# RWKV time mixing on one core: a second GpSimd product for each early unit, and the mix vectors transposed between two halves of unit 0

## The chip, the core and the metric

The kernel runs on one core of a Trainium2 chip. A core has five engines with a queue of instructions each: PE (TensorE, the matrix engine, with its weight loads shown as PEld), DVE (VectorE), ACT (ScalarE), POOL (GpSimd) and SP (SyncE, which only issues DMAs here). They run side by side and wait for one another through semaphores. The metric is the device time of one execution in microseconds (us); lower is better.

## What is computed

For x of shape 16 x 2048 x 256 and with x_prev the same rows shifted by one position in the sequence (zero in front), the reference is, cut to what reaches the output:

```python
xv = x * time_mix_v + x_prev * (1 - time_mix_v)
xr = x * time_mix_r + x_prev * (1 - time_mix_r)
v = xv.reshape(-1, d_model) @ value_weight
r = xr.reshape(-1, d_model) @ receptance_weight
out = ((1.0 / (1.0 + np.exp(-r))) * v) @ output_weight
```

The key path (time_mix_k, key_weight) is computed in the reference but its result isn't used, and the kernel leaves it out.

## The kernel before

The 16 x 2048 rows are cut into 64 units of 512 rows, four to a batch element ("batch" below). All work is on x transposed: the 256 features lie on the 128 partitions in two halves, called ko 0 and ko 1, and the 512 rows of a unit lie along the free dimension.

Mixing is rewritten so that it costs little: with c = 1/time_mix - 1, the mix is time_mix * (c * x_prev + x), and time_mix is multiplied into the weights once, at the start. For each unit and for each of R (m = 0) and V (m = 1) there remain two **products**, c * x_prev for ko 0 and for ko 1 (128x512 each; `scale` on DVE, line 258, `scale_pool` on POOL, line 268, `scale_act` on ACT, line 515), and one **sum** over both halves (`add`, 128x1024, DVE, line 280). The shifted x_prev is the transposed x one slot earlier; the first slot of a unit (or of a batch) has to be filled by a small copy, `wrap_slots` (lines 427 and 428).

The loop over g at line 523 does, for unit g, on PE: R's four matmuls (`project`, line 288, into psum_r), transposes of later units (line 209, 8 for each unit, into ps_t), V's four matmuls (line 288, into psum_v), and the eight output matmuls of the unit before (line 312, into psum_o). psum_v has one buffer. ACT takes the sigmoid of psum_r (line 536), copies transposed tiles from ps_t (line 225) and the output from psum_o (line 346). DVE multiplies the sigmoid with psum_v into z_sb (line 581). Beside this each engine prepares the mix of later units.

The order is written out by hand: the framework adds semaphores but moves nothing. Tables filled in lines 483 to 510 say in which iteration which piece is made:

- `sums[g]`: DVE's sums ahead of the z_sb product of iteration g. The last of these is `last`.
- `held[g]`: DVE's sums behind the z_sb product of iteration g.
- `products[g]`: DVE's products ahead of the sums.
- `pooled[g]`: pieces whose second product (ko 1) POOL does. They are issued after the z_sb product in program order, and made to wait for `last` (`scale_pool(p, last)`, line 589, with the reason "one at a time").

For units 3 to 7, R's sum is in `sums` of the iteration before the unit, and V's is in `held` there (unit 7: both in `sums`). Before the change, DVE makes three of the four products of each of units 3 to 8 in the iteration before (both of R, the first of V; for unit 8's R two iterations before), and POOL makes V's second product one iteration earlier still. Unit 2's V gets its second product from ACT (line 564). From unit 10 on (`PAIRS`), two units are mixed together, and POOL makes the second product of both R and V as 128x1024; this stays as it is.

In the steady order DVE runs, per iteration: products, R's sum of unit g + 1, z_sb of unit g, V's sum of unit g + 1. PE's V matmuls of unit g + 1 need that last sum. POOL runs, per iteration: the wrap copy of unit g + 2 (line 428), the second product (line 268), then the issue of a load of x (line 114) and a two-column copy (line 427).

At the start, PE runs 21 matmuls on zeros (line 153), a 4x128 transpose of the mix vectors (`coefficients`, line 171), the transposes of unit 0 in two halves (line 232; the half with the later rows first, into psum_r, the other into psum_v), 10 more matmuls on zeros, and then unit 0. DVE turns the transposed mix vectors into time_mix, 1 - time_mix and c (lines 175 to 184), copies unit 0's shifted slot (line 239), and scales the weights (lines 455, 462, 471).

Of the kernel before, what the change touches and what calls it, by code (L numbers as in the profile page):

```python
# [15 lines left out]
def kernel(  # L16
# [44 lines left out]
    START_T = [1, 3, 5, 6, 7, 9, 11, 12]  # L61
    AHEAD = 6
    PAIRS = 10
    WARM = 21
    WARM2 = 10

    consts = ctx.enter_context(tc.tile_pool(name="consts", bufs=1))
# [11 lines left out]
    SYNC = mybir.DependencyInfo(mybir.DependencyClass.Sync, mybir.DependencyReason.DATA)  # L79
# [70 lines left out]
    def warm_up(n):  # L150
        ps = ps_t_pool.tile([P, P], FP32, name="ps_t")
        for _ in range(n):
            nc.tensor.matmul(out=ps, lhsT=zeros, rhs=zeros, start=True, stop=True)  # L153

    warm_up(WARM)

# [12 lines left out]
    def coefficients():  # L169
        ps = ps_o_pool.tile([P, 2, KO], FP32, name="psum_o")  # L170
        nc.tensor.transpose(
            out=ps.rearrange("p m k -> p (m k)"), in_=tm_rows, identity=ident_f[: 2 * KO, : 2 * KO]
        )
        tm = consts.tile([P, 2, KO], FP32)
        nc.vector.tensor_copy(out=tm, in_=ps)
        nc.vector.tensor_scalar(
            out=tms, in0=tm, scalar1=0.0, scalar2=1e-30, op0=ALU.is_equal, op1=ALU.mult
        )
        nc.vector.tensor_tensor(out=tms, in0=tms, in1=tm, op=ALU.add)
        nc.vector.tensor_scalar(  # L180
            out=tm_prev, in0=tm, scalar1=-1.0, scalar2=1.0, op0=ALU.mult, op1=ALU.add
        )
        nc.vector.reciprocal(c_sb, tms)
        nc.vector.tensor_scalar(out=c_sb, in0=c_sb, scalar1=-1.0, scalar2=None, op0=ALU.add)

    coefficients()

    def by_dma(b, lo, hi, after=None):

        op = nc.sync.dma_start_transpose(  # L190
            out=xt[b][:, 1 + lo : 1 + hi].rearrange("p j k c -> p (j k) c"),
            in_=x_bf[b][:, lo:hi].rearrange("p j d -> p (j d)"),
        )
        if after is not None:
            tc.add_manual_dep(op.ins, after.ins.name, SYNC, reason="not beside a load")
# [31 lines left out]
    def first_transposes():  # L227
        def half(h, pool, name):
            ps = pool.tile([P, UJ, KO, P], FP32, name=name)
            for jj in range(H):  # L230
                for ko in range(KO):
                    nc.tensor.transpose(  # L232
                        out=ps[:, jj, ko],
                        in_=x_unit[:, 0, h * H + jj, ko * P : (ko + 1) * P],
                        identity=ident_f,
                    )
            nc.scalar.copy(out=xt[0][:, 1 + h * H : 1 + h * H + H], in_=ps[:, 0:H])
            if h == 1:
                nc.vector.tensor_copy(out=xt[0][:, 0, :, 1:P], in_=ps[:, H - 1, :, 0 : P - 1])

        half(1, ps_r_pool, "psum_r")
        half(0, ps_v_pool, "psum_v")

    def slots(piece, off=0):

        b, _, lo, hi = piece
        j = lo // P + (lo // TU if b < BYUNIT else 0) + off
        return slice(j, j + (hi - lo) // P)

    def mixed(piece):  # L250
        b, m, lo, hi = piece
        j = lo // P % (2 * UJ)
        return mix[(b * S + lo) // (2 * TU)][:, m, j : j + (hi - lo) // P]
# [9 lines left out]
                op0=ALU.mult,  # L263
            )

    def scale_pool(piece, after):
        b, m, _, _ = piece
        op = nc.gpsimd.tensor_scalar(  # L268
            out=mixed(piece)[:, :, 1],
            in0=xt[b][:, slots(piece), 1],  # L270
            scalar1=c_sb[:, m, 1:2],
            scalar2=1.0,
            op0=ALU.mult,
            op1=ALU.mult,
        )
        tc.add_manual_dep(op.ins, after.ins.name, SYNC, reason="one at a time")

    def add(piece):
        b = piece[0]
# [121 lines left out]
    def tile_for(b):  # L401

        if b not in mix:
            mix[b] = mixpool.tile([P, 2, 2 * UJ, KO, P], BF16, name="mix")

    def pieces(g):

        b, e = divmod(g, UB)
        tile_for(g // 2)
        return [(b, m, e * TU, (e + 1) * TU) for m in range(2)]  # L410
# [75 lines left out]
    pooled = {g: [] for g in range(-1, NU)}  # L486
# [12 lines left out]
    for u in range(2, NU):  # L499
        paired = u >= PAIRS  # L500
        if paired and u % 2:
            continue
        for m, (b, _, lo, hi) in enumerate(pieces(u)):
            w = first[u][m]
            group = (b, m, lo, hi + TU if paired else hi)
            if paired or m == 1 and w > 1 and u != PAIRS - 1:
                products[w].append((group, (0,)))
                pooled[w - 1].append(group)
            else:
                products[w].append((group, (0,) if u == 2 and m == 1 else (0, 1)))  # L510

    def scale_act(piece, kos):
        b, m, _, _ = piece
        for ko in kos:
            nc.scalar.activation(  # L515
                out=mixed(piece)[:, :, ko],
                in_=xt[b][:, slots(piece), ko],
                func=ACT.Copy,
                scale=c_sb[:, m, ko : ko + 1],
            )  # L520

    z_prev2 = z_prev = None
    for g in range(NU - 1):
        ps_r = ps_r_pool.tile([P, KO, TU], FP32, name="psum_r")
        if g == 0:
            project_unmixed(ps_r, 0)
            advance(1)
            project_unmixed(ps_r, 1)
            for ko in range(KO):
                wrap_slots(pieces(1)[0], ko)  # L530
                scale(pieces(1)[0], (ko,))
            last = add(pieces(1)[0])
        else:
            project(ps_r, g, 0)
        s_sb = zpool.tile([P, KO, TU], BF16, name="s_sb")
        nc.scalar.activation(out=s_sb, in_=ps_r, func=ACT.Sigmoid)  # L536
        advance(START_T[g] if g < len(START_T) else g + LOOK - (g == CROSS - 1))
        for b in range(B - 5, B):
            if g == max(UB * (b - 2) - 1, CROSS + (b > B - 5)):
                new_xt(b)  # L540
                if b == B - 5:
                    for pair in kept.pop(g):
                        store(nc.sync, *pair, after=half_load)
                    by_dma(b, J - UJ, J, last_load)
                    by_dma(b, 0, J - UJ, last_load)
                else:
                    by_dma(b, 0, J)
                for pair in kept.pop(g, []):
                    store(nc.sync, *pair)
            if g == UB * (b - 1) + 1:  # L550
                nc.scalar.copy(out=xt[b][:, 0, :, 1:P], in_=xt[b][:, J, :, 0 : P - 1])
        if LATE_O < g < NU - 2:
            output(g - 2, z_prev2)
        for p in products.get(g + 1, []):
            if g >= FREE and p[0][1] == 1:
                scale_act(p[0], (0,))
        for p in [q for q, _ in products[g]] + pooled[g]:
            last_unit_of = p[3] // TU - 1
            need = last_unit_of if p[0] < BYUNIT else min(last_unit_of + 1, UB - 1)
            assert UB * p[0] + need < tnext, (g, p, tnext)  # L560
            if g > AHEAD or p not in pooled[g]:
                wrap_slots(p)
        if g == 1:
            scale_act(pieces(2)[1], (1,))
        for p, kos in products[g]:
            if not (g - 1 >= FREE and p[1] == 1):
                scale(p, kos)
        for p in sums[g]:
            last = add(p)
        for p in pooled[g]:  # L570
            if p[0] >= BYUNIT:
                wrap_slots(p)
        ps_v = ps_v_pool.tile([P, KO, TU], FP32, name="psum_v")
        project(ps_v, g, 1)
        if g == 0:
            scale_act(pieces(1)[1], (0,))
            advance(2)
        z_sb = zpool.tile([P, KO, TU], BF16, name="z_sb")
        n = TU // 2 if g == NU - 2 else TU
        for c in range(0, TU, n):  # L580
            nc.vector.tensor_tensor(  # L581
                out=z_sb[:, :, c : c + n],
                in0=s_sb[:, :, c : c + n],
                in1=ps_v[:, :, c : c + n],
                op=ALU.mult,
            )
        for p in pooled[g]:
            wrap_slots(p, after=last)
            scale_pool(p, last)
        for p in held[g]:  # L590
            add(p)
        if z_prev is not None and not LATE_O <= g < NU - 3:
            output(g - 1, z_prev)
        if g == 1:
            advance(4)
        z_prev2, z_prev = z_prev, z_sb
# [31 lines left out]
```

## Time and profile before

| | |
|---|---|
| median of 4 runs | 203.15 us (202.12, 202.53, 203.76, 203.76) |
| the profiled execution's own time | 202.59 us |
| its span, first to last instruction | 200.5 us |
| granted TensorE clock over the span | 1.000 |
| DMA, mean | 286 GB/s |

The profile is of one execution. It has a page with the busy time of each engine, the chain of work that ended last and the costliest groups of instructions, and the trace behind it answers by view: the waits (who waited for whom), the timeline (instructions in order of time: start, duration, engine, line, operation, out<-in, shape, how many; in brackets the idle time in front and what ended it), the chain of waits in order of time, the DMA issues, and sums over windows. Times in the timeline count from the start of the span. Of a run of equal instructions the timeline gives one row, with the time from the first start to the last end. DVE starts an instruction some 0.08 us before the one in front is recorded as ended, so that spacing and duration differ.

### The profile page before, as it was taken

The numbers are of one execution on the slowest core, as the hardware profiler recorded it, in microseconds if no ns is written. First come the engines' busy times: TensorE is split into PE (matmuls) and PEld (weight loads), VectorE is DVE, ScalarE is ACT, GpSimd is POOL, SyncE is SP. The second block draws the span as 40 slices with busy tenths as digits, with TensorE's granted clock in tenths as the row PEclk, the third lists the DMA queues.
The fourth block names the chain that finished last, engine by engine and source line by source line (L and its number), as shares of the span: only waits on it lengthen the run. The fifth ranks groups of instructions, "written<-read, shape, count | busy, mean of one in ns | idle before, by whom it ended". The sixth has DMA issues, their size and how long they took to land.

```text
span 200.5 us, 3886 instructions
## 1 busy us (share of the span) xinstructions
PE 195.6 (98%) x1420; PEld 125.9 (63%) x1420; DVE 186.2 (93%) x296; ACT 180.1 (90%) x202; POOL 83.7 (42%) x115
## 2 busy tenths in 40 slices
PE   7999999999999999999999999999999999999993
PEld 6666675666666666666666666655666565555671
DVE  2799999999999999999999999999999999999982
ACT  3599899999999999999999999899999999999982
POOL 1656572443533534425434354443344444444200
PEclk9999999999999999999999999999999999999999
DMA  5999999999999999999999999899999999999575
GB/s 163 295 162 215 232 281 274 278 280 273 293 312 294 289 273 289 289 280 286 286 280 317 301 406 295 288 187 207 298 269 415 332 218 267 418 418 413 226 310 213
DMA packets 32298, 57.26 MB, mean 286 GB/s; under 512 B 21780, under 2 KB 23064, under 8 KB 28312
## 3 DMA queue, kind: packets, MB, share of 16 engines
q1 hardware_dynamic: 28208, 40.77, 59.1%
q0 software_dynamic: 3920, 16.12, 40.1%
q8 instruction: 11, 0.18, 0.3%
q10 hardware_dynamic: 152, 0.13, 0.2%
q14 instruction: 7, 0.06, 0.1%
HBM read 34.34 MB, written 33.55 MB: 339 GB/s over the span
## 4 chain that ended last, share of the span: by engine, by line
PE 88%; DVE 5%; ACT 3%; issue 2%; POOL 0%; DVEq 0%
PE psum_v L288 25%; PE psum_o L312 25%; PE psum_r L288 24%; PE ps_t L209 8%; DVE z_sb L581 2%; PE ps_t L153 2%; DVE mix L280 2%; PE ps_t L312 1%; ACT s_sb L536 1%; DVE mix L258 1%; PE psum_r L302 1%; ACT mix L515 1%; PE psum_v L232 1%; PE psum_r L232 1%; ACT xt L225 1%
## 5 line engine op out<-in xcount | busy, mean ns | idle before, releaser
L268 POOL TENSOR_SCALAR mix<-xt,c_sb 128x1024 bf16<-128x1024 bf16 (+1 forms) x55 | 61.0, 1109 | 92.6 <-DVE mix L280 81.9
L581 DVE TENSOR_TENSOR z_sb<-s_sb,psum_v 128x1024 bf16<-128x1024 bf16 (+1 forms) x64 | 76.8, 1201 | 3.5 <-PE psum_v L288 1.5
L280 DVE TENSOR_TENSOR mix<-mix,xt 128x1024 bf16<-128x1024 bf16 x112 | 77.0, 697 | 1.6
L288 PEld LDWEIGHTS <-w_bf 128*128 128x128 bf16 x516 | 48.7, 98 | 38.4 <-issue 0.7
L536 ACT ACTIVATE s_sb<-psum_r 128x1024 bf16<-128x1024 f32 x63 | 65.0, 1031 | 3.5 <-PE psum_r L288 2.7
L346 ACT COPY o_sb<-psum_o 128x1024 f32<-128x1024 f32 x60 | 61.1, 1018 | 7.1 <-PE psum_o L312 7.1
L288 PE MATMUL psum_v<-mix,w_bf 128*128 128x512 bf16 (+1 forms) x256 | 65.3, 377 | 0.3 <-DVE z_sb L581 0.2
L288 PE MATMUL psum_r<-mix,w_bf 128*128 128x512 bf16 (+1 forms) x252 | 64.2, 377 | 0.1
L312 PE MATMUL psum_o<-wo_bf,z_sb 128*128 128x256 bf16 x486 | 63.2, 272 | 0.0
L312 PEld LDWEIGHTS <-z_sb 128*128 128x128 bf16 x512 | 49.8, 98 | 20.4 <-issue 1.4
L225 ACT COPY xt<-ps_t 128x1024 bf16<-128x1024 bf16 x36 | 36.6, 1030 | 0.0
L209 PEld LDWEIGHTS <-x_bf 128*128 128x128 bf16 x328 | 21.4, 98 | 9.1 <-POOL xt_first L427 0.5
L209 PE MATMUL ps_t<-ident,x_bf 128*128 128x128 bf16 x328 | 24.5, 219 | 0.1
L258 DVE TENSOR_SCALAR mix<-xt,c_sb 128x1024 bf16<-128x1024 bf16 (+1 forms) x49 | 22.1, 459 | 0.0
L515 ACT ACTIVATE mix<-xt,c_sb 128x1024 bf16<-128x1024 bf16 x12 | 13.9, 1157 | 0.0
L280 DVE TENSOR_TENSOR mix<-mix,xt_first 128x1024 bf16<-128x1024 bf16 x15 | 10.6, 709 | 0.1
L114 POOL DMA_DIRECT2D x_bf<-in_x_dram x13 | 8.5, 656 | 0.0
L258 DVE TENSOR_SCALAR mix<-xt_first,c_sb 128x512 bf16<-128x512 bf16 x22 | 6.6, 348 | 0.2
L225 ACT COPY xt_first<-ps_t 128x1024 bf16<-128x1024 bf16 x5 | 5.2, 1036 | 0.0
L153 PE MATMUL ps_t<-zeros 128*128 128x128 bf16 x31 | 3.7, 311 | 1.0 <-DVE zeros L90 1.0
L268 POOL TENSOR_SCALAR mix<-xt_first,c_sb 128x512 bf16<-128x512 bf16 x6 | 4.1, 686 | 0.6
L428 POOL COPY xt_first<-xt_first 128x254 bf16<-128x254 bf16 x5 | 2.0, 393 | 5.5 <-DVE mix L280 5.4
(66 smaller groups left out, 52.1 us busy)
## 6 DMA issues: line engine op xcount, KB each, us to landing
out_dram<-o_sb SPq DMA_DIRECT2D x28, 1024.0 KB, 14.4
x_bf<-in_x_dram POOLq DMA_DIRECT2D x13, 1024.0 KB, 24.6
out_dram<-o_sb SPq DMA_DIRECT2D x4, 512.0 KB, 2.8
out_dram<-o_sb SPq DMA_DIRECT2D x6, 256.0 KB, 2.5
x_bf<-in_x_dram POOLq DMA_DIRECT2D x5, 256.0 KB, 7.1
o_sb<-in_x_dram SPq DMA_DIRECT2D x2, 512.0 KB, 5.3
x_bf<-in_x_dram POOLq DMA_DIRECT2D x2, 512.0 KB, 11.1
o_sb<-in_x_dram SPq DMA_DIRECT2D x2, 256.0 KB, 3.1
```

The lines of the kernel that those rows point to most:

```text
L114: return nc.gpsimd.dma_start(out=x_bf[b], in_=rows(b), max_dma_last_dim=run)
L209: nc.tensor.transpose(out=ps[:, jj], in_=src[:, jj, ko * P : (ko + 1) * P], identity=idn)
L225: nc.scalar.copy(out=xt[b][:, j0 : j0 + UJ], in_=ps)
L258: nc.vector.tensor_scalar(out=mixed(piece)[:, :, ko], in0=xt[b][:, slots(piece), ko], scalar1=c_sb[:, m, ko : ko + 1], scalar2=None, op0=A ...
L268: op = nc.gpsimd.tensor_scalar(out=mixed(piece)[:, :, 1], in0=xt[b][:, slots(piece), 1], scalar1=c_sb[:, m, 1:2], scalar2=1.0, op0=ALU.mul ...
L280: return nc.vector.tensor_tensor(out=mixed(piece), in0=mixed(piece), in1=xt[b][:, slots(piece, 1)], op=ALU.add)
L288: nc.tensor.matmul(out=ps[:, mo, :], lhsT=w_bf[:, m, ko, mo * P : (mo + 1) * P], rhs=mixed((b, m, e * TU + lo, e * TU + hi))[:, :, ko], st ...
L312: nc.tensor.matmul(out=ps[:, slot, :], lhsT=z[:, ko, jj * P : (jj + 1) * P], rhs=wo_bf[:, ko, :], start=(ko == 0), stop=(ko == KO - 1),)
L346: nc.scalar.copy(out=o_sb[b][:, j0 : j0 + UJ, :], in_=ps)
L515: nc.scalar.activation(out=mixed(piece)[:, :, ko], in_=xt[b][:, slots(piece), ko], func=ACT.Copy, scale=c_sb[:, m, ko : ko + 1],)
L536: nc.scalar.activation(out=s_sb, in_=ps_r, func=ACT.Sigmoid)
L581: nc.vector.tensor_tensor(out=z_sb[:, :, c : c + n], in0=s_sb[:, :, c : c + n], in1=ps_v[:, :, c : c + n], op=ALU.mult,)
```

## The change

Four edits:

1. For units 3 to 8, R's second product goes from DVE to POOL, ahead of V's second product in the same iteration (for unit 8 as the code says: in iteration 6, where V's of unit 8 also is).
2. Unit 2's V gets its second product from POOL instead of ACT, with no added wait on `last`.
3. `coefficients()` is called between the two halves of unit 0's transposes, instead of ahead of both. On DVE its instructions stay in the same order, ahead of the copy into unit 0's first slot.
4. 23 matmuls on zeros at the start in place of 21.

POOL's queue is then, in the iterations of units 2 to 5: wrap copy, R's second product, V's second product, issue of the load, two-column copy. In DVE's queue one `scale` is gone in each, and R's sum waits for POOL's product.

```diff
-    WARM = 21
+    WARM = 23
...
-    coefficients()
-
...
             nc.scalar.copy(out=xt[0][:, 1 + h * H : 1 + h * H + H], in_=ps[:, 0:H])
             if h == 1:
+                coefficients()
                 nc.vector.tensor_copy(out=xt[0][:, 0, :, 1:P], in_=ps[:, H - 1, :, 0 : P - 1])
...
-    def scale_pool(piece, after):
+    def scale_pool(piece, after=None):
...
-        tc.add_manual_dep(op.ins, after.ins.name, SYNC, reason="one at a time")
+        if after is not None:
+            tc.add_manual_dep(op.ins, after.ins.name, SYNC, reason="one at a time")
...
-            if paired or m == 1 and w > 1 and u != PAIRS - 1:
+            if paired or w > 1 and u != PAIRS - 1:
                 products[w].append((group, (0,)))
-                pooled[w - 1].append(group)
+                at = w if m == 0 and u == AHEAD + 2 else w - 1
+                pooled[at].insert(0 if m == 0 else len(pooled[at]), group)
             else:
                 products[w].append((group, (0,) if u == 2 and m == 1 else (0, 1)))
...
-            if g > AHEAD or p not in pooled[g]:
+            if g > AHEAD or p not in pooled[g] or p == pieces(AHEAD + 2)[0]:
                 wrap_slots(p)
         if g == 1:
-            scale_act(pieces(2)[1], (1,))
+            scale_pool(pieces(2)[1])
```

## The prediction

> **What bounds the kernel now.** I read the busy times first, then who waited for whom, then the timeline from 0 to 37 us.
>
> ```profile
> PE 195.6 (98%) x1420; PEld 125.9 (63%) x1420; DVE 186.2 (93%) x296; ACT 180.1 (90%) x202; POOL 83.7 (42%) x115
> ```
>
> ```profile
> PEld L288 <- DVE mix L280: 0.4, 2, 0.2
> ...
> PE psum_v L288 <- DVE z_sb L581: 0.2, 1, 0.2
> ```
>
> PE has work for 98% of the span, and its waits are short: a gain can come only from the few places where it stands still. The chain of waits has PE alone from 33.40 us on, with a V projection every 3.05 us (40.10, 43.15, 46.20). Before that the spacing shows the losses. An iteration with 8 transposes should take 3.05 us: the ones from 16.41 and from 19.66 take 3.25 (0.20 lost each), the one from 29.91 takes 3.49 (0.44 lost). One with 16 transposes takes 3.50 (22.91 to 26.42), without a wait. So 0.84 us is all that the product edits can win. The timeline shows what ends these waits:
>
> ```profile
> 21.63 0.68 POOL L268 TENSOR_SCALAR mix<-xt_first,c_sb 128x512 bf16<-128x512 bf16 x1
> 22.06 0.80 DVE L280 TENSOR_TENSOR mix<-mix,xt_first 128x1024 bf16<-128x1024 bf16 x1
> ...
> 22.78 0.88 DVE L258 TENSOR_SCALAR mix<-xt_first,c_sb 128x512 bf16<-128x512 bf16 x3
> 22.91 0.55 PEld L288 LDWEIGHTS <-w_bf 128*128 128x128 bf16 x4 [0.20 <-DVE mix L280]
> ...
> 23.04 0.20 POOL L427 COPY xt_first<-xt_first 128x2 bf16<-128x2 bf16 x1
> ...
> 25.61 0.69 DVE L280 TENSOR_TENSOR mix<-mix,xt_first 128x1024 bf16<-128x1024 bf16 x1
> ...
> 27.03 0.73 POOL L427 COPY xt_first<-xt_first 128x2 bf16<-128x2 bf16 x1
> 27.04 0.67 DVE L280 TENSOR_TENSOR mix<-mix,xt_first 128x1024 bf16<-128x1024 bf16 x1
> ...
> 33.40 1.02 PE L288 MATMUL psum_v<-mix,w_bf 128*128 128x512 bf16 x4 [0.25 <-DVE z_sb L581]
> ```
>
> DVE has no gap here; V's sum ends at 22.86 and PE goes on at 22.91. So DVE is the bound of these iterations. The second thing to see is that a DVE sum and a POOL operation take turns. The sum at 22.06 begins 0.25 us before POOL's product ends (22.31) and takes 0.80, not the 0.69 of 25.61, which meets no product: it ends 0.55 after the product. The sums at 15.52 and 28.76 end 0.54 after theirs. The other way round, POOL's two-column copy takes 0.20 at 23.04, but 0.73 at 27.03, where it meets a sum, and ends 0.05 after it. The z_sb product isn't stretched (20.93: 1.21 beside a product).
>
> At the start the rows to see are those that a DMA ends:
>
> ```profile
> 3.34 0.18 PEld L171 LDWEIGHTS psum_o<-ident_f,tm_rows 4*128 4x128 f32 x1 [0.20 <-issue]
> ...
> 4.67 0.72 PEld L232 LDWEIGHTS psum_v<-ident_f,o_sb 128*128 128x128 f32 x4 [0.42 <-DMA o_sb<-in_x_dram]
> ...
> 6.23 0.62 DVE L455 TENSOR_SCALAR w_prev<-w_f,tm_prev 128x256 bf16<-128x256 f32 x2 [0.51 <-DMA w_f<-n_receptance_weight_dram]
> ...
> 7.84 0.86 PEld L209 LDWEIGHTS ps_t<-ident_f,o_sb 128*128 128x128 f32 x8 [0.32 <-DMA o_sb<-in_x_dram]
> ```
>
> **The start (edits 3 and 4): 0.** Matmuls on zeros follow each other every 0.107 us (21 from 0.99, the last at 3.10), so 23 end at about 3.42, 0.1 before unit 0's first half began (3.53). That half can begin at most 0.1 earlier; the second begins at 4.67 as before, when its DMA lands. The mix vectors' transpose falls behind the first half, whose last transpose starts at 4.23 and takes 0.21: at 4.44, in PE's idle time before 4.67. DVE's first step came 0.30 after L171 (3.64) and the six steps end 0.98 later (4.62). Now 4.74 to 5.72, then the 0.42 copy of line 239 to 6.14. The weight scaling at 6.23 waits for a DMA: cover 0.09. If that is gone, each 0.1 of lateness costs 0.1, until the DMA at 7.84 covers again; I bound it by +0.3 (the whole shift) and -0.1 (the earlier first half), and take 0: 4.67, 6.23 and 7.84 are set by DMAs.
>
> PE runs 128-column matmuls every 0.107 us up to 6.54 and every 0.056 from 12.48 (8 in 0.44), while the granted clock stands at 1.00 throughout: it speeds up somewhere after 6.6. The Trainium skill ("TensorE: Matmul & The Clock Gate", Part 1) says that the clock doubles after a window of about 3.4 us of activity, free-running; closing PE's pause at 3.2 could then move the step one window earlier. By that rule the sum would still not change, since the DMA rows above hold 4.67, 6.23 and 7.84.
>
> **Unit 2's V product, ACT to POOL: +0.28 on DVE.** On ACT it took 0.73 at 14.25; the output copy behind it (14.88) waited for matmuls that end at 14.83, so ACT wins 0.05 at most, and I count 0. On POOL it waits for DVE's copy (ends 12.89) and starts 0.13 later, as POOL does behind `last`: 13.02 to 13.70. That is beside DVE's three products, 13.00 to 13.88. The trace has no such pair of full size. Bounds: 0, from the two-column copy at 23.04, which neither waits nor slows the products beside it (0.88 for three, as at 13.00 without POOL); and the sum's behaviour, turns. I take turns: the copy has 2 columns where the product has 512, and the sum is the only row of full size. A sum whose turn comes has 0.54 of its 0.69 left, so 0.15 is behind it; a product (0.34) has 0.19 left. The second one (13.27) then ends at 13.70 + 0.19 = 13.89, not 13.61: +0.28, and z_sb of iteration 1 goes from 14.39 to 14.67. Its end, 15.88, is still ahead of the V projection at 16.41.
>
> **R's product, DVE to POOL.** Removed from DVE: one product, 0.26 of spacing, per iteration; without contention the iteration falls from 3.25 to 2.99, under PE's 3.05. Added on POOL: 0.65 (a product to the next operation: 18.38 to 19.03). From the start of z_sb, by rows 20.93 to 22.86: `last` ends at 0.07 (21.00), the wrap copy starts 0.14 later (21.14), R's product 0.49 after that and lasts 0.68: it ends at 1.38, where V's did. V's sum is asked for at 1.13 and ends at 1.38 + 0.54 = 1.92. V's product has to wait for that sum; a blocked copy of 2 columns ends 0.05 after, and 512 columns more cost 0.43 (1.117 for 1024 against 0.686 for 512): 2.40. DVE's first product, asked for at 1.84, ends 0.19 after that (2.59); the second starts 0.08 before, R's sum 0.26 later, the next z_sb 0.60 later: 3.37 per iteration instead of 3.25. PE's V projection starts 0.05 after V's sum. From 14.67:
>
> - iteration 1: V's sum ends 16.59; projection 16.64 (16.41 before);
> - 2: z_sb 18.04, sum 19.96, projection 20.01 (19.66);
> - 3: z_sb 21.41, sum 23.33, projection 23.38 (22.91);
> - 4: z_sb 24.78; the sum at 26.70 is ahead of PE, which takes 3.51: 26.89 (26.42);
> - 5: z_sb 28.15, sum 30.07; PE 26.89 + 3.49 = 30.38 (29.91);
> - 6: from the sum to z_sb it was 29.56 to 32.13, 2.57; two products less, -0.52; V's product delays the copy behind the sum by 0.41 (0.48 + 0.06 - 0.13): z_sb at 32.53, ends at 33.74, projection 0.06 later: 33.80 (33.40).
>
> Unit 8's products start 0.17 after `last` (as at 32.38): R's ends about 33.46, ahead of its sum (33.66); V's makes that sum end near 34.65, and z_sb of iteration 7 then ends at 37.2, before PE wants psum_v at 37.29. From there PE is the bound again. Sum: **+0.40 us**, from 202.59 to 202.99 for the profiled execution. That one lies 0.56 under the median, so on the median's scale 203.15 + 0.40 = 203.55.
>
> The Trainium skill ("SBUF — State Buffer", Who interferes with whom) speaks against this edit: DVE's two-port modes, and sums of two SBUF tensors, share one port pair with GpSimd, and whoever comes first keeps it for the whole instruction. By it the turns hold for DVE's products too (+0.40, or more if products follow each other without a gap for the sum); by the row at 23.04 they don't, and case C holds. The rows of the sums agree with it.
>
> **What is queued behind.** On POOL the load of 15.77 goes out about 1.3 us later (behind V's product, which ends at 17.07). Loads issued in the first 20 us land a median 15.1 later with the DMA engines busy, so it stands in line anyway; at worst it lands 1.3 later than 30.87, still before PE's transposes of that batch at 32.55. SP's stores move with ACT's copies by PE's own shift. DVE's new wait, R's sum for POOL's R product (done an iteration earlier), costs 0.
>
> **The rivals.**
> - **B, slower:** POOL goes from R's product to V's without letting the waiting sum in. Place: V's sum, iterations 1 to 6. Its end moves from 1.92 to 1.38 + 0.65 + 0.54 = 2.57, after which the two products run free: 3.61 per iteration. The same walk gives projections at 17.29, 20.95, 24.61, 28.27, 31.93 and 35.20: +1.80, 204.95. It decides if V's product starts its reading before the sum gets its turn. For it: POOL starts an operation 0.04 before the last one ends. Against: 15.10, where a memset follows the product and the sum goes by the product's end; but a memset reads nothing.
> - **C, faster:** DVE's products don't mind POOL. V's product then runs beside them, and 0.19 and 0.44 are won (19.66 stays, since z_sb at 17.76 also waits for the sigmoid, which ends at 17.72): -0.6, 202.55; all of it would be -0.84, 202.3. For it the row at 23.04.
> - **D:** the start goes wrong, 0.3 on top of A: 203.85.
>
> **How the numbers follow.** A 0.45, B 0.20, C 0.30, D 0.05. Likeliest: 203.55 (its own range 203.25 to 203.85, from 0 at 13.00 to a second turn lost). The range over the cases is 202.3 to 205.0, from C's whole gain to B; runs above and below are the 2 in 10 left out. A change of 1% is about what a measurement of this kernel can tell from none: under 201.1 faster, over 205.2 slower. C with a lucky run, 0.03; B with unit 2's whole product in the way (0.68, not 0.28: 205.35) and D, 0.12; the same, 0.85.
>
> **What would show it.** Right: sums at line 280 of 0.8 us or more beside two products in a row on POOL; the first product behind V's sum stretched; V's product about 0.9 to 1.1 long; V projections 3.37 apart from 16.6 to 23.4. B: V's sum over 1.3 us long. C: DVE gaps between 19 and 33 us, projections 3.05 apart. Wrong at the start: L455 later than 6.3 with no DMA in front.

## The result and the profile after

The changed kernel takes 204.33 us (median of 32 runs, 204.08 to 206.18); the kernel before has 202.85 us in the runs beside it. The ratio is 1.0081, 95% interval 1.0066 to 1.0095: slower by 1.3 to 1.9 us. The forecast had 203.55 us, so the sign and "within 1%" hold, and the time lies in the wide range, but 0.5 us above the likeliest case's own range. The added time shows the miss better: the forecast had +0.40 us on a kernel before of 203.15 us (the median of 4 runs), which has 202.85 us in 51 runs, and the measured addition is some four times as large. The profiled execution is the slowest of the 32 (206.18 us, span 204.2); what sets it apart from the other profiles of this study lies in its first 13 us, as shown below.

The busy times and the chain of waits of the changed kernel:

```profile
PE 197.3 (97%) x1422; PEld 127.1 (62%) x1422; DVE 188.2 (92%) x290; ACT 179.7 (88%) x201; POOL 90.4 (44%) x122
...
PE 76%; DVE 13%; issue 4%; ACT 3%; DMA 2%; POOL 0%; SPq 0%; DVEq 0%; POOLq 0%
```

POOL has 6.7 us more and DVE, which gave six products away, has 2.0 us more, not less: 0.26 us each was taken from it, and more was put on by waiting. In the chain, DVE carries 13%. The waits of TensorE on DVE, which were 0.4 and 0.2 us before (second view shown in the prediction); the columns are us in total, times, and the longest:

```profile
PEld L288 <- DVE mix L280: 1.7, 4, 0.5
...
PE psum_v L288 <- DVE mix L280: 0.8, 3, 0.4
...
PE psum_v L288 <- DVE z_sb L582: 0.7, 2, 0.5
```

Since each iteration makes one z_sb on DVE, the steps from one z_sb to the next show where the time went. The numbers are differences of the starts in the timelines; "forecast" is the prediction's walk, "unit 2", "R" and "none" are three experiments told below (edit 2 alone, edit 1 alone, and R's product done by nobody).

| step, us | before | forecast | changed | unit 2 | R | none |
|---|---|---|---|---|---|---|
| 0 to 1 | 3.46 | 3.73 | 3.90 | 3.90 | 3.46 | 3.48 |
| 1 to 2 | 3.36 | 3.37 | 3.46 | 3.27 | 3.67 | 3.34 |
| 2 to 3 | 3.17 | 3.37 | 3.42 | 3.25 | 3.31 | 3.04 |
| 3 to 4 | 3.55 | 3.37 | 3.54 | 3.53 | 3.53 | 3.05 |
| 4 to 5 | 3.16 | 3.37 | 3.31 | 3.18 | 3.31 | 3.49 |
| 5 to 6 | 4.50 | 4.38 | 4.65 | 4.51 | 4.65 | 3.87 |
| 6 to 7 | 3.12 | 3.47 | 3.46 | 3.12 | 3.46 | 3.12 |
| 7 to 8 | 3.36 | - | 3.70 | 3.35 | 3.35 | 3.36 |
| 8 to 9 | 3.08 | - | 3.08 | 3.07 | 3.07 | 3.08 |
| z_sb(0) to z_sb(9) | 30.75 | - | 32.50 | 31.18 | 31.81 | 29.83 |

Behind z_sb(9) little differs: from there to the end, each profile of this study (14 of them) has 160.8 to 161.1 us left of its own time (160.9 before, 160.8 changed; 161.0 and 161.1 in the two runs with added products, whose next step is 0.36 us longer). So the change costs 1.75 us between z_sb(0) and z_sb(9); everything else is the start.

The timeline of one iteration of the changed kernel, the one from z_sb(2) (start, us, engine, line, operation, count, and in brackets the idle time ahead of it and what ended it):

```profile
20.26 1.21 DVE L582 TENSOR_TENSOR z_sb<-s_sb,psum_v 128x1024 bf16<-128x1024 bf16 x1
...
20.97 1.78 POOL L267 TENSOR_SCALAR mix<-xt_first,c_sb 128x512 bf16<-128x512 bf16 x2
...
21.39 0.80 DVE L280 TENSOR_TENSOR mix<-mix,xt_first 128x1024 bf16<-128x1024 bf16 x1
...
22.12 1.04 DVE L257 TENSOR_SCALAR mix<-xt_first,c_sb 128x512 bf16<-128x512 bf16 x2
22.25 0.55 PEld L288 LDWEIGHTS <-w_bf 128*128 128x128 bf16 x4 [0.41 <-DVE mix L280]
...
23.68 1.21 DVE L582 TENSOR_TENSOR z_sb<-s_sb,psum_v 128x1024 bf16<-128x1024 bf16 x1
```

The mechanism is the one forecast. Counted from z_sb's start at 20.26: POOL's pair begins at 0.71; V's sum is asked for at 1.13, gets its turn between R's and V's product (0.80 us, not 0.68) and ends at 1.93; the pair ends at 2.49 (1.78 us for two products that need 0.68 each); the first scale behind the sum takes 0.78 us of the 1.04 for two, instead of 0.34; the next z_sb begins at 3.42. TensorE's weight loads stand 0.41 us for V's sum.

### The profile page after: what moved, and what is told of

The parts are those of the page before. It is cut to its first block, busy times and chain, and to the rows that moved or that the text cites. A ratio compares the mean times of both kernels' runs of the same rounds, so it can differ in the third digit from the quotient of the medians.

```text
span 204.2 us, 3898 instructions
## 1 busy us (share of the span) xinstructions
PE 197.3 (97%) x1422; PEld 127.1 (62%) x1422; DVE 188.2 (92%) x290; ACT 179.7 (88%) x201; POOL 90.4 (44%) x122
## 4 chain that ended last, share of the span: by engine, by line
PE 76%; DVE 13%; issue 4%; ACT 3%; DMA 2%; POOL 0%; SPq 0%; DVEq 0%; POOLq 0%
PE psum_v L288 22%; PE psum_o L312 22%; PE psum_r L288 21%; PE ps_t L207 6%; DVE z_sb L582 5%; DVE mix L280 5%; DVE mix L257 3%; DMA o_sb<-in_x_dram 2%; PE ps_t L312 1%; ACT s_sb L537 1%; ACT xt L223 1%; PE psum_r L302 1%; PE psum_v L230 1%; PE ps_t L153 1%; ACT mix L516 1%
## 5 line engine op out<-in xcount | busy, mean ns | idle before, releaser
L267 POOL TENSOR_SCALAR mix<-xt,c_sb 128x1024 bf16<-128x1024 bf16 (+1 forms) x56 | 61.7, 1102 | 91.0 <-DVE mix L280 85.0
L267 POOL TENSOR_SCALAR mix<-xt_first,c_sb 128x512 bf16<-128x512 bf16 x12 | 10.6, 892 | 2.9 <-DVE mix L280 1.3
L257 DVE TENSOR_SCALAR mix<-xt_first,c_sb 128x512 bf16<-128x512 bf16 x17 | 8.2, 522 | 0.2
L216 ACT CAST xt_first<-ps_t 128x512 bf16<-128x512 f32 x4 | 2.2, 586 | 2.6 <-PE ps_t L207 2.6
```

Source lines behind the costliest of these rows:

```text
L257: nc.vector.tensor_scalar(out=mixed(piece)[:, :, ko], in0=xt[b][:, slots(piece), ko], scalar1=c_sb[:, m, ko : ko + 1], scalar2=None, op0=A ...
L267: op = nc.gpsimd.tensor_scalar(out=mixed(piece)[:, :, 1], in0=xt[b][:, slots(piece), 1], scalar1=c_sb[:, m, 1:2], scalar2=1.0, op0=ALU.mul ...
```

## The experiments

Twelve kernels were run, each timed in five rounds beside the kernel before. Differences in us below are the ratio's, times about 203; the profile of each gives the steps.

### The edits one by one

The start alone:

```diff
-    WARM = 21
+    WARM = 23
...
-    coefficients()
...
             if h == 1:
+                coefficients()
```

> Edits 3 and 4 alone (coefficients between the halves of unit 0, two more warm-up matmuls); the products stay where the kernel before has them. The profile of the changed kernel begins its first z_sb 1.97 us later than the profile of before, its own time is the highest of its runs, and the median of all runs grew by about 1.5 us. Theory P (the products cost all of it, and the late head is one execution's bad luck): no change, within 0.3 us of before, and z_sb(0) at 10.9 to 11.2 us in the profile unless unit 0's second half lands late again. Theory H (the late head belongs to edits 3 and 4, and the products cost the 0.4 us of the prediction): slower by 1.0 to 1.2 us, z_sb(0) at 12 us or later with TensorE's transposes 0.107 us apart until about 10 us.

Measured: 202.82 us, ratio 0.9999 (0.9975 to 1.0023). z_sb(0) at 11.27, steps as before to 0.01 us. Theory P holds for the start: no cost is seen, to within 0.5 us (z_sb(0) is a little later than the 10.9 to 11.2 that was expected).

Then why does the changed kernel's own profile begin z_sb 1.97 us later? The timeline of its start:

```profile
5.51 0.72 PEld L230 LDWEIGHTS psum_v<-ident_f,o_sb 128*128 128x128 f32 x4 [0.74 <-DMA o_sb<-in_x_dram]
...
7.01 0.62 DVE L455 TENSOR_SCALAR w_prev<-w_f,tm_prev 128x256 bf16<-128x256 f32 x2 [0.80 <-DMA w_f<-n_receptance_weight_dram]
...
9.20 1.58 PE L207 MATMUL ps_t<-ident_f,o_sb 128*128 128x128 f32 x8
```

In this execution the second half of unit 0 landed late (5.51, where before had 4.67), the receptance weights too (7.01, where before had 6.23), and TensorE ran at half its pace unusually long: of the 8 transposes at 9.20 the first six follow each other every 0.213 us, the last every 0.109. The two landings belong to the execution, not to the edit: head_only has 4.57 and 6.04 in these two places. The long slow phase can't be settled by so few profiles: of the four with the start edits, two have it (this one and wrap_early below), of the ten without none. If the edits make it likelier, its cost is inside the 0.5 us.

The products alone (the diff of the change without the two start edits):

> Edits 1 and 2 alone (R's second product of units 3 to 8 and V's second product of unit 2 on POOL); head as before. Theory P: slower by 1.3 to 1.7 us, the whole difference of the changed kernel. Theory H: slower by 0.3 to 0.5 us. In the profile, from z_sb(1) on, the starts of psum_v should stand 3.4 to 3.5 us apart by theory P, as in the profile of the changed kernel; the prediction had 3.37.

Measured: 204.44 us, ratio 1.0071 (1.0048 to 1.0095), +1.0 to +1.9 us. All nine steps agree with the changed kernel's to 0.01 us. Theory H falls, theory P holds.

Unit 2's product alone:

```diff
-    def scale_pool(piece, after):
+    def scale_pool(piece, after=None):
...
         if g == 1:
-            scale_act(pieces(2)[1], (1,))
+            scale_pool(pieces(2)[1])
```

> Edit 2 alone: V's second product of unit 2 on POOL instead of ACT. The prediction has +0.28 us on z_sb(1); the changed kernel's profile shows the DVE scale beside it at 0.789 us instead of 0.343, which is 0.45. If all of it reaches the end: +0.3 to +0.5 us. If a later slack takes it up (TensorE waits 0.2 to 0.4 us several times behind it in the profile of before, so DVE is what paces there): 0 to +0.1 us only if the pace is TensorE's.

Measured: 203.15 us, ratio 1.0010 (0.9990 to 1.0031); step 0 to 1 is 3.90 instead of 3.46, and the way to z_sb(9) is 0.43 us longer. The time alone wouldn't tell it from nothing; the step does. The same place in the changed kernel's timeline:

```profile
14.97 1.31 DVE L257 TENSOR_SCALAR mix<-xt_first,c_sb 128x512 bf16<-128x512 bf16 x3
15.04 0.85 POOL L267 TENSOR_SCALAR mix<-xt_first,c_sb 128x512 bf16<-128x512 bf16 x1 [1.02 <-DVE xt_first L428]
```

POOL's product begins 0.07 us behind the first of three scales. It meets that one first, so it takes 0.85 us and not 0.68, and the second scale has to wait for all of it: three scales take 1.31 us, where three without POOL take 0.88.

R's products alone (the change without the start edits and with `scale_act(pieces(2)[1], (1,))` kept):

> Edit 1 alone: R's second product of units 3 to 8 on POOL, V's second product of unit 2 stays on ACT. Theory P: +0.9 to +1.2 us (the product edits together less edit 2's 0.3 to 0.5). Prediction as it stands: about +0.1 to +0.4 us, since it has 3.37 us for an iteration and TensorE as the bound again from 33.8 us. If the loss behind 33.8 us belongs to edit 1, TensorE waits 0.5 us or more near z_sb(8) in this profile as well.

Measured: 203.42 us, ratio 1.0025 (1.0002 to 1.0047), +0.04 to +0.95 us; the steps add up to 1.06 us. Of these, 0.2 us in step 1 to 2 is probably not the edit's, and half of it comes back in the next step: this execution began early (z_sb(0) at 10.69), and TensorE then stood 0.57 us at 11.77 ahead of transposes whose load had fully landed at 12.41 (at 12.12 in r_3to6 below, where the two steps are 3.46 and 3.42). TensorE's stall for z_sb(8) (from one matmul's start to the next, beyond the usual distance) is 0.28 us here and 0.63 in the changed kernel. That difference, 0.35 us in step 7 to 8, is in neither single edit, and led to the next two runs.

### A product that starts late

The timeline of the changed kernel around z_sb(7):

```profile
38.63 1.21 DVE L582 TENSOR_TENSOR z_sb<-s_sb,psum_v 128x1024 bf16<-128x1024 bf16 x1
...
39.23 1.11 POOL L267 TENSOR_SCALAR mix<-xt,c_sb 128x1024 bf16<-128x1024 bf16 x1 [1.79 <-DVE mix L280]
...
39.76 1.12 DVE L280 TENSOR_TENSOR mix<-mix,xt 128x1024 bf16<-128x1024 bf16 x1
...
43.60 1.02 PE L288 MATMUL psum_v<-mix,w_bf 128*128 128x512 bf16 x4 [0.46 <-DVE z_sb L582]
```

POOL's first product of 1024 columns begins 0.60 us behind z_sb(7)'s start; with R alone the same product begins 0.25 us behind it (36.33 against 36.08). The semaphore it waits for comes 0.11 us behind z_sb's start in both. Late as it is, it meets V's sum, which takes 1.12 us; z_sb(8) is late and TensorE is idle for 0.46 us ahead of 43.60.

```diff
+    one_more = consts.tile([P, 1], FP32)
...
         if g == 1:
             scale_pool(pieces(2)[1])
+            nc.gpsimd.memset(one_more, 0.0)
```

> The changed kernel with one more instruction on POOL, a memset of one column of a tile that nothing reads, right after unit 2's product. In the profiles of the changed kernel and of the products alone, POOL's first product of 1024 columns (39.23 and 38.08 us) starts 0.49 us after its last semaphore instead of 0.14 us, and the step from z_sb(7) to z_sb(8) is 3.70 us; with R alone on POOL, one instruction fewer ahead of it, it starts 0.14 us after, and the step is 3.35 us. Theory F (the late start sits at a place in POOL's stream of instructions, not in the data): the extra instruction moves another instruction onto that place, the product starts 0.14 us after its semaphore, the step falls to about 3.35 us and the time by 0.3 us against the changed kernel, to about +1.2 us on before. Theory G (it belongs to the data, the transfers or DVE's traffic at that moment): the step stays at 3.70 us and the time at +1.5 us or a little more.

Its timeline around z_sb(7):

```profile
36.53 1.21 DVE L584 TENSOR_TENSOR z_sb<-s_sb,psum_v 128x1024 bf16<-128x1024 bf16 x1
...
36.78 1.11 POOL L268 TENSOR_SCALAR mix<-xt,c_sb 128x1024 bf16<-128x1024 bf16 x1 [1.45 <-DVE mix L281]
...
37.66 0.78 DVE L281 TENSOR_TENSOR mix<-mix,xt 128x1024 bf16<-128x1024 bf16 x1
```

The product now begins 0.25 us behind z_sb, V's sum takes 0.78 and the step is 3.35. Theory G falls. The time doesn't show it: 204.80 us, ratio 1.0076 (1.0048 to 1.0104), an interval as wide as the effect; the profiled execution alone took 203.85 us, its early start (z_sb(0) at 10.73) included.

The same memset in the kernel with R alone:

> Edit 1 alone (R's products of units 3 to 8 on POOL) with the same extra one-column memset on POOL, so that POOL's stream is as long as in the changed kernel. Theory F: the product of 1024 columns starts 0.49 us after its semaphore, the step from z_sb(7) to z_sb(8) grows from 3.35 to 3.70 us, and the time by 0.3 us, from +0.56 to about +0.9 us on before. Theory G: nothing changes, +0.5 to +0.6 us.

Measured: 203.88 us, ratio 1.0038 (1.0008 to 1.0068); step 7 to 8 stays 3.35. This expectation failed, by its count: I had the stream as long as the changed kernel's, but unit 2's product brings a wait instruction of its own, two records on POOL, and the memset is one. Counted in the trace with its waits, the late one is the 69th POOL record in the changed kernel, in the products alone, and in the run with added products below (there a wait, 0.45 us behind the record ahead of it); in r_plus_one the product of 1024 columns is the 68th, and in after_plus_one the 70th, and both are in time. So the place in the stream decides, as theory F has it; what the engine does at that place, no run here shows.

### What a second product on POOL costs, and what it relieves

R's second product done by nobody, so that the output is not the reference's (units 3 to 8; the start and unit 2 as in the kernel before):

```diff
-            out=mixed(piece), in0=mixed(piece), in1=xt[b][:, slots(piece, 1)], op=ALU.add
+            out=mixed(piece),
+            in0=xt[b][:, slots(piece)] if piece in unscaled else mixed(piece),
...
+    unscaled += [pieces(u)[0] for u in range(3, AHEAD + 3)]
...
-            scale_pool(p, last)
+            if p not in unscaled:
+                scale_pool(p, last)
```

> R's second product of units 3 to 8 is left out altogether: neither DVE nor POOL does it, and the sum of those pieces reads the plain x instead, so R's input of units 3 to 8 is not the reference's. Everything else of edit 1 stays; V's product of unit 2 on ACT. It shows what the relief of DVE is worth without the load on POOL. Theory T: DVE sheds 0.26 us per iteration and meets no turns; TensorE's stalls of 0.20, 0.19 and 0.41 us go: 0.3 to 0.8 us faster than before. If DVE's load were not what paces units 3 to 8: within 0.1 us of before.

Measured: 201.93 us, ratio 0.9942 (0.9916 to 0.9967), 0.7 to 1.7 us faster; the steps add up to 0.92 us less. Its timeline behind z_sb(3):

```profile
21.76 0.69 POOL L269 TENSOR_SCALAR mix<-xt_first,c_sb 128x512 bf16<-128x512 bf16 x1
...
22.32 0.69 DVE L282 TENSOR_TENSOR mix<-mix,xt_first 128x1024 bf16<-128x1024 bf16 x1
...
22.93 0.61 DVE L259 TENSOR_SCALAR mix<-xt_first,c_sb 128x512 bf16<-128x512 bf16 x2
```

One product on POOL, ending 0.13 us into V's sum (21.76 + 0.69 = 22.45 against 22.32): the sum takes 0.69 and the two scales 0.61 together, nothing is stretched, and the step is 3.05, TensorE's pace. Theory T holds: the relief is real, and by the steps it is a little more than the 0.84 us that the prediction allowed at most.

The opposite: DVE keeps all its products, and POOL gets one more for each unit, for nobody.

```diff
             wrap_slots(p, after=last)
+            if p in twice:
...
+                op = nc.gpsimd.tensor_scalar(
+                    out=spare[:, :, 1],
+                    in0=xt[b][:, slots(p), 1],
...
             scale_pool(p, last)
```

> The kernel before, DVE keeping every product, and one more POOL product per iteration for units 3 to 8, into a tile that nothing reads, ahead of V's product as in the changed kernel (work is added, none of the reference's is left out). Nobody waits for it. Theory T (POOL's second product costs by taking turns with DVE's sum and first scale): DVE's sum gets 0.12 us longer and its first scale 0.45 us longer in each iteration, with none of its work taken off; the six iterations are 3.5 to 3.8 us long and the time grows by 1.5 to 3 us, far more than R's products on POOL cost alone (0.56 us). Theory W (the cost in the changed kernel is that R's sum waits for POOL's product): an extra product that nobody waits for costs 0 to 0.3 us.

Its timeline behind z_sb(3), with the extra product at line 593:

```profile
23.74 0.69 POOL L593 TENSOR_SCALAR spare<-xt_first,c_sb 128x512 bf16<-128x512 bf16 x1
...
24.17 0.80 DVE L281 TENSOR_TENSOR mix<-mix,xt_first 128x1024 bf16<-128x1024 bf16 x1
...
24.41 1.11 POOL L269 TENSOR_SCALAR mix<-xt_first,c_sb 128x512 bf16<-128x512 bf16 x1
24.89 0.78 DVE L259 TENSOR_SCALAR mix<-xt_first,c_sb 128x512 bf16<-128x512 bf16 x1
```

Measured: 205.45 us (6 runs), ratio 1.0112 (1.0076 to 1.0149), +1.5 to +3.0 us, the steps +2.82. The sum takes 0.80, the scale behind it 0.78, V's product 1.11, as in the changed kernel, though no instruction waits for the extra product. Theory T holds, theory W falls: the cost is not that R's sum waits for POOL's data, it is the turns.

With half the columns (`spare[:, 0:H, 1]`):

> The kernel before with POOL's extra product per iteration (units 3 to 8, into a tile that nothing reads) cut from 512 to 256 columns. With 512 columns the time grew by 2.3 us (ratio 1.0112) and the steps of z_sb 1 to 6 were 0.50, 0.64, 0.26, 0.64 and 0.43 us longer than before. Theory T (the price is the length of POOL's work that overhangs z_sb): some 0.3 us of POOL's work less in each iteration, so 0.15 to 0.3 us less per step, +0.8 to +1.5 us on before. If the price goes by the number of POOL's products and not by their length (a price per meeting): still +2 us or more.

The same stretch of its timeline:

```profile
22.36 0.47 POOL L593 TENSOR_SCALAR spare<-xt_first,c_sb 128x256 bf16<-128x256 bf16 x1
...
22.79 0.68 DVE L281 TENSOR_TENSOR mix<-mix,xt_first 128x1024 bf16<-128x1024 bf16 x1
22.82 1.39 POOL L269 TENSOR_SCALAR mix<-xt_first,c_sb 128x512 bf16<-128x512 bf16 x1
...
23.39 0.96 DVE L259 TENSOR_SCALAR mix<-xt_first,c_sb 128x512 bf16<-128x512 bf16 x2
```

Measured: 204.34 us, ratio 1.0055 (1.0028 to 1.0083), +0.6 to +1.7 us, the steps +1.31: less than half of the full product's 2.82, as theory T had it. Here the sum is ahead of V's product by 0.03 us and isn't stretched; V's product takes 1.39 us because it lets the sum and the first scale (0.34 us) through, and then holds the second (0.70 us). The price goes with the length, but the meeting doesn't vanish: it moves from the sum to the scale.

### Where it is lost behind 33 us

```diff
-            if paired or w > 1 and u != PAIRS - 1:
+            if paired or w > 1 and u != PAIRS - 1 and (m == 1 or u < 7):
```

> Edit 1 for units 3 to 6 alone; units 7 and 8 keep R's second product on DVE, V's product of unit 2 stays on ACT. With units 3 to 8 on POOL (0.56 us slower) the steps of z_sb were longer than before by 0.31, 0.14, 0, 0.15 (z_sb 1 to 5), 0.15 (5 to 6) and 0.34 us (6 to 7). Theory L (the two last steps, behind 33 us, are lost to units 7 and 8): the steps from z_sb(5) to (6) and (6) to (7) go back to 4.50 and 3.12 us, and the time comes to within 0.2 us of before. Theory M (all of it is one delay carried along): the last two steps stay long and the time stays at +0.4 us or more.

Measured: 203.54 us, ratio 1.0023 (0.9994 to 1.0051). Step 6 to 7 goes back to 3.12, as theory L says; step 5 to 6 doesn't, it is 4.74 against 4.50 before. So each theory fails in one half, and the time can't decide between them. The timeline of that step, first of the kernel before, then of this one:

```profile
25.53 1.47 POOL L114 DMA_DIRECT2D x_bf<-in_x_dram  x2
...
27.63 1.21 DVE L581 TENSOR_TENSOR z_sb<-s_sb,psum_v 128x1024 bf16<-128x1024 bf16 x1
...
28.34 0.68 POOL L268 TENSOR_SCALAR mix<-xt_first,c_sb 128x512 bf16<-128x512 bf16 x1
```

```profile
27.10 1.47 POOL L114 DMA_DIRECT2D x_bf<-in_x_dram  x2
...
28.07 1.21 DVE L583 TENSOR_TENSOR z_sb<-s_sb,psum_v 128x1024 bf16<-128x1024 bf16 x1
...
29.21 0.68 DVE L281 TENSOR_TENSOR mix<-mix,xt_first 128x1024 bf16<-128x1024 bf16 x1
29.23 1.27 POOL L268 TENSOR_SCALAR mix<-xt_first,c_sb 128x512 bf16<-128x512 bf16 x1
...
29.94 1.22 DVE L258 TENSOR_SCALAR mix<-xt_first,c_sb 128x512 bf16<-128x512 bf16 x3
```

Before, POOL's two load issues end 0.63 us ahead of z_sb(5), and V's product begins 0.71 us into it. Here they stand behind two products and end 0.50 us into z_sb(5), and V's product begins 1.16 us into it, 0.02 us behind V's sum: it takes 1.27 us and holds the scales behind it (1.22 us for three). The changed kernel's timeline has the same, with two products:

```profile
30.52 1.21 DVE L582 TENSOR_TENSOR z_sb<-s_sb,psum_v 128x1024 bf16<-128x1024 bf16 x1
...
31.66 0.68 DVE L280 TENSOR_TENSOR mix<-mix,xt_first 128x1024 bf16<-128x1024 bf16 x1
31.68 1.96 POOL L267 TENSOR_SCALAR mix<-xt_first,c_sb 128x512 bf16<-128x512 bf16 x2
...
32.39 1.40 DVE L257 TENSOR_SCALAR mix<-xt_first,c_sb 128x512 bf16<-128x512 bf16 x2
...
34.70 0.55 PEld L288 LDWEIGHTS <-w_bf 128*128 128x128 bf16 x4 [0.42 <-DVE mix L280]
```

The pair begins at 31.68, again 1.16 us into z_sb(5). Two scales take 1.40 us and R's sum ends late for TensorE (0.42 us at 34.70). Two products fewer on DVE (0.52 us) bring a step that is 0.15 us longer.

### Two versions meant to be faster

POOL's wrap copy without its wait for the sum, so that the pair begins earlier:

```diff
-        if after is not None:
+        if after is not None and not at_once:
             tc.add_manual_dep(op.ins, after.ins.name, SYNC, reason="one at a time")
...
-            wrap_slots(p, after=last)
+            wrap_slots(p, after=last, at_once=True)
```

> The changed kernel, in which POOL's copy of the wrapped column ahead of the two products no longer waits for V's sum, only for ACT's copy of x, whose data it needs. In the changed kernel the order on POOL is sum's end, 0.14 us, copy 0.39 us, product, product, so that the pair starts 0.7 us into z_sb and overhangs its end by 0.6 to 0.9 us. Theory T (the cost is the part of the pair that overhangs z_sb, by turns with DVE's sum and scale): where ACT's copy is in time the pair starts up to 0.5 us earlier, the scale behind the sum is less stretched, and the time falls by 0.3 to 0.8 us against the changed kernel, to +0.7 to +1.2 us on before. If the early copy meets V's sum and stretches that by as much, or ACT's copy comes too late for it: no change, +1.5 us.

Its timeline from z_sb(3):

```profile
23.48 1.21 DVE L582 TENSOR_TENSOR z_sb<-s_sb,psum_v 128x1024 bf16<-128x1024 bf16 x1
23.73 1.35 POOL L267 TENSOR_SCALAR mix<-xt_first,c_sb 128x512 bf16<-128x512 bf16 x2 [0.93 <-DVE mix L280]
...
24.61 1.02 DVE L280 TENSOR_TENSOR mix<-mix,xt_first 128x1024 bf16<-128x1024 bf16 x1
```

Measured: 203.86 us, ratio 1.0053 (1.0024 to 1.0082), in theory T's range, but overlapping the changed kernel's interval; steps 32.10 in all against 32.50. Of these 0.40 us, 0.35 is the late product alone, so that the earlier pair itself won next to nothing. The pair begins 0.25 us into z_sb and runs without a break (1.35 us), but V's sum, asked for while the second product already ran, now takes 1.02 us: POOL's two products do keep the sum out when the second has begun first. Steps 4 to 5 (3.16), 5 to 6 (4.22) and 7 to 8 (3.35) are shorter; the last is the late product again, POOL's stream having changed. Steps 0 to 1 (4.09), 2 to 3 (3.52) and 3 to 4 (3.75) are longer, where the early copy meets a scale or a sum. So the reason that theory T gave, the overhang alone, was too simple.

The same edit on the kernel before:

> The kernel before with the one edit that took about 0.5 us off the changed kernel: POOL's copy of the wrapped column no longer waits for V's sum. One product follows it, so POOL's work (0.24 to 0.93 us into z_sb) then lies wholly inside z_sb's 1.21 us and meets neither V's sum nor a scale; in the kernel before it overhangs z_sb by 0.18 us, and the sum there takes 0.71 to 0.81 us instead of 0.68. If that small overhang is what stands between this kernel and a shorter iteration: 0.1 to 0.4 us faster. If the early copy stretches DVE's second scale as in the changed kernel (0.34 to 0.66 us in two of its iterations): 0.1 to 0.5 us slower. Within 0.1 us: the two cancel.

Its timeline behind z_sb(3), the product ending at 21.77:

```profile
21.73 0.76 POOL L114 DMA_DIRECT2D x_bf<-in_x_dram  x1
...
21.97 0.90 DVE L280 TENSOR_TENSOR mix<-mix,xt_first 128x1024 bf16<-128x1024 bf16 x1
...
22.79 1.00 DVE L258 TENSOR_SCALAR mix<-xt_first,c_sb 128x512 bf16<-128x512 bf16 x3
22.86 0.52 POOL L428 COPY xt_first<-xt_first 128x254 bf16<-128x254 bf16 x1
```

Measured: 203.35 us, ratio 1.0024 (1.0001 to 1.0048), steps 31.56 against 30.75. The product now lies inside z_sb, and it is slower all the same: the copy's turns cost more (0.52 us for the copy, 1.00 for three scales). V's sum takes 0.90 us here, while the only other work on POOL is the load issue at 21.73. The largest loss, step 4 to 5 (3.74 against 3.16), has one scale of 0.61 us beside a load issue. Whether load issues take turns too isn't settled: another sum beside one takes 0.68. No version here beats the kernel before with the whole computation.

## Why the prediction was right or wrong, step by step

- **Start, 0:** right as far as the times tell, and with luck. head_only has 0.9999, but to within 0.5 us only. The cover was thinner than the forecast's 0.09 us: DVE is done 0.06 us ahead of the weight scaling in head_only, and in after_plus_one only as it begins. In the 14 profiles the weights land anywhere from 5.80 to 6.99 us, while DVE's chain with the start edits ends at 5.98 to 6.23; where they land early, it would be late.
- **Mechanism A, turns:** right, with its shape. Sums 0.80 beside a pair, V's product 1.10, the first scale 0.78, V's sum ahead of V's product: as listed under "what would show it", with V projections 3.46 and 3.42 apart where it had 3.37.
- **Unit 2, +0.28:** the mechanism right, the size short: +0.44. The step that failed is "On POOL it ... 13.02 to 13.70": it gave POOL's product its free length of 0.68, but the product meets the first scale before it blocks the second, and takes 0.85.
- **Iteration, 3.37:** 3.46, 3.42 and 3.31 measured where DVE paces (1 to 2, 2 to 3, 4 to 5). Step 3 to 4 is 3.54, 0.17 us longer than the walk had it and as long as before: z_sb(4) begins 0.72 us behind R's sum instead of 0.60, and the last semaphore that it waits for is that of ScalarE's copy, which ends at 27.04. The walk left this wait out. The walk from z_sb's start is 0.01 us off at the sum's end and 0.09 off at the end of V's product.
- **Step 5 to 6, 4.38:** failed, 4.65. The prediction let the load issues on POOL go out later and called that harmless, since it looked only at what the loads feed. What stands behind them on POOL is the next pair: it comes 0.45 us later than V's product in the kernel before and meets the sum and two scales, not one.
- **Step 6 to 7, 3.47:** right, 3.46, and so is that TensorE doesn't wait for z_sb(7).
- **"From there PE is the bound again":** failed. The walk stopped one iteration early. It let the delay of z_sb(7), 0.7 us, vanish but for 0.40, but z_sb(8) is bound to z_sb(7) by a DVE step of 3.36 us, longer than TensorE's 3.05; in the kernel before z_sb(8) ends (39.82) only 0.12 us ahead of the projection that wants it (39.94):

```profile
38.61 1.21 DVE L581 TENSOR_TENSOR z_sb<-s_sb,psum_v 128x1024 bf16<-128x1024 bf16 x1
...
39.94 1.03 PE L288 MATMUL psum_v<-mix,w_bf 128*128 128x512 bf16 x4
```

  With R alone TensorE waits 0.28 us there. The late product adds 0.35 us, which the profile of before could not show.
- **The sum, +0.40:** the steps give +1.75. Of the 1.35 us between them, 0.67 has come up by z_sb(7), in the terms above (unit 2, the iterations, step 3 to 4, step 5 to 6); 0.35 is the late product; 0.34 is the part of z_sb(7)'s delay that the walk let vanish. No single step made the forecast too small.
- **Rival B (no turn for the sum):** not in iterations 1 to 5 of the changed kernel, where no sum takes over 0.80 us. It happens when the second product has begun before the sum asks: in wrap_early (sums of 1.01 to 1.03 us), and once in the changed kernel, with unit 8's pair, where the prediction had allowed for it:

```profile
35.42 1.36 POOL L267 TENSOR_SCALAR mix<-xt,c_sb 128x512 bf16<-128x512 bf16 x2 [1.77 <-DVE mix L280]
...
36.30 1.01 DVE L280 TENSOR_TENSOR mix<-mix,xt 128x1024 bf16<-128x1024 bf16 x1
```

- **Rival C (scales don't mind POOL):** false, the two-column copy was the wrong row to go by; its gain exists only with the product left out. **Rival D (0.3 us lost at the start):** no sign of it, but the interval of head_only doesn't exclude 0.3 us.

The Trainium skill ("SBUF — State Buffer", Who interferes with whom) says that DVE and GpSimd share a pair of SBUF ports under an exclusive lock. The rows agree: 0.78 for a scale of 0.34, 0.85 for a product of 0.68, 0.80 to 1.12 for a sum of 0.68, and z_sb, which reads one operand from PSUM, at 1.21 throughout. The lock belongs to the instruction, not to the engine: a waiting sum gets in between two products that stand back to back (0.80 us) if it asks before the second begins, and waits for both (1.01 and 1.02 us) if it asks after.

## What to carry to other kernels

That GpSimd is idle doesn't make work moved to it from DVE free: here 0.26 us taken off DVE per iteration came back as 0.3 to 0.5 us of turns (2.0 us between R's products on POOL and done by nobody, 2.8 us for the added ones, over six units), so look for the stretch in which DVE does something that doesn't take turns (z_sb here) and move no more than fits into it. One product fitted here; no order tried above had room for a second. Follow a delay until an iteration has slack for it in its own rows, not until the first engine is in time again. And when a queue gets longer, ask what compute stands behind its DMA issues, not only what the DMAs feed.

## What the hardware showed beyond the forecast

- **A fixed late place in GpSimd's stream.** The 69th POOL record, waits counted, starts some 0.35 us later than what released it explains. It is a product in the changed kernel, the products alone and before_wrap_early (0.49 to 0.52 us behind the start of its wait's record instead of 0.14 or 0.15), and a wait in both runs with added products and in r_3to6. In the other profiles it stands behind a longer wait or a load issue, and nothing shows. One instruction more or fewer ahead of it moves a different one there.
- **TensorE's pace.** At the start, matmuls of 128 columns come every 0.107 us, later every 0.056, while the granted clock reads 1.00 throughout. The first matmul at full pace is at 4.6 us in the products alone, 4.7 in head_only, 7.4 in before and 10.3 in the changed kernel. Twelve of the fourteen executions lie between 4.6 and 7.4 us; the two with the latest z_sb(0) (12.91 in the changed kernel, 12.40 in wrap_early) changed last, at 10.3 and 9.4. The Trainium skill ("TensorE: Matmul & The Clock Gate", Part 1) calls the window free-running and the count of slow matmuls variable from run to run, and that there is a spread agrees; its size doesn't, since the page has the step around 4 us into sustained activity, give or take 0.5 us, and here, with TensorE pausing in between, 5.7 us lie between the earliest and the latest. Its use in the prediction, that two more warm-up matmuls could bring the step earlier, isn't shown: it is 4.6 us in one execution with 21 and 4.7 us in one with 23.
- **Time and profile.** In the 14 profiled executions z_sb(0) begins anywhere from 10.6 to 12.9 us, while the steps behind it repeat to about 0.01 us in the two pairs that share their products (before and head_only, the changed kernel and the products alone). A term of 0.35 us was settled by a profile, and not by eleven timed runs.
